# Attention of a two-layer hybrid block: the last ten (head, query block) units of each layer as five two-head units, and the row of maxima in one pass

## The chip, the cores and the metric

The kernel is one program on one core of a Trainium2 chip. The metric is device time in microseconds, from launch to end. All tensors are fp32 in DRAM. TensorE multiplies, VectorE and ScalarE read its results from PSUM, GpSimd does work on SBUF, and SyncE (SP) issues nearly all DMAs.

## The reference

Two layers (`DEPTH = 2`) work on 256 context tokens followed by 2048 latent tokens of width 1024. Each layer is normalised and modulated, projected, and run through three groups of heads in parallel: a bidirectional SSD (6 heads), a bidirectional gated delta rule (4 heads), and attention with 6 query heads of 64 over 2 key/value heads. The mixed result is projected back and added. In the second layer only the latent rows are needed. The attention is plain:

```
def block(qi):
    s = jnp.einsum('bqhgd,bkhd->bhgqk', qi, k).astype(jnp.float32) * scale
    pr = jax.nn.softmax(s, axis=-1).astype(v.dtype)
    return jnp.einsum('bhgqk,bkhd->bqhgd', pr, v)
```

Latent queries see all 2304 keys (18 tiles of 128). Context queries see the 256 context keys, and are computed in layer 0 only.

## The kernel before, in words

The order of a layer is: projections (L389 to L487) in three groups of tokens; gating, preparation and triangular solve of the delta rule (`gdn_pre`, `gdn_solve`); the SSD (`ssd_states`, `ssd_out`); the serial delta-rule chain (`gdn_chain`, 18 steps of two half steps each); the output projection (`load_mix`, `project`, `finish`). Attention is a generator whose units the program emits around the chain: eight units before it, the rest behind it. The order in which each engine gets its instructions is made by the framework's scheduler, which plays the program through with a timeline of its own and gives instructions emitted earlier the higher priority; `tc.high_priority()` raises what stands in it. Each engine then works through its list in that order and waits on semaphores.

A unit of attention is one head with 512 queries against 18 key tiles. There are 24 units of latent queries in each layer (4 query blocks by 6 heads), listed in `big`, and six small ones of context queries in layer 0. A unit has two parts.

`unit_max` (L516) finds the maxima of the scores. For each of 4 query tiles it makes five pieces of scores with the queries as the stationary operand (L531, four of 512 keys and one of 256), reduces each along the keys on VectorE (L533), reduces the five (L535), negates (L536), and turns the four columns of negated maxima into one row by fp32 matmuls against the identity (L541), which VectorE copies into row 64 of `qm` (L542). `qm` holds the first 64 rows of the queries' high and low parts (copied by GpSimd, L522) with that row below; `klo` has a row of ones there. So the second score matmul of `unit_main` subtracts the maximum as it adds the correction for the split of the keys.

`unit_main` (L545) goes over the 18 key tiles: two score matmuls in fp32r (L562, L563) into a PSUM slot, the exponential on ScalarE (L565) into `pe`, and the product with V into `po` (L556), one PSUM bank of its own. V has 65 columns per head; the 65th is ones, so row 64 (or 0) of `po` is the sum of the exponentials. Up to unit 12 that product is one fp32 matmul, which the hardware runs as two instructions. From unit 13 on, `pe` is split into a rounded part `ph` on ScalarE (L570) and a rest `pl` on VectorE (L571), V is split once into `vh[0]` and `vh[1]`, and the product is three fp32r matmuls.

While unit i runs its main part, the maxima of unit i+1 are advanced step by step (`adv`), so that they are spread over its first 14 key tiles. Scores, maxima and the row of maxima share PSUM slots: three banks in `ps_s`, and for the first units a fourth in `ps_x`. After the unit, `po` is copied (L579), and its rows go out by DMA to `mx_d` and `sm_d`; after six units `inv` takes the reciprocals of the sums.

The chain (`gdn_chain`, `load`, `prep`, `step`) loads its data two steps ahead (`kqc`, `acv`, L1034 to L1055), scales `kqc` on VectorE (L1060), and passes a state through TensorE, VectorE and ScalarE in each half step. `behind(mm, prev)` (L1002) fixes the order of two matmuls without a semaphore.

`ssd_states` (L789) has matmuls with 64 output columns, the two groups written to the lower and the upper 64 partitions of one PSUM bank. `identr` is the identity in fp32r, used to transpose in the projections (L326).

## Time and profile before

| | |
|---|---|
| runs | 3998.72, 4003.42, 4008.57 us; median 4003.42 |
| the profiled execution | 3989.31 us, of which the span of instructions is 3987.5 |
| TensorE busy | 3758.9 us, 94% of the span |
| VectorE, ScalarE, GpSimd busy | 2704.5 (68%), 1799.1 (45%), 1347.3 (34%) |
| granted TensorE clock, mean | 0.975 |

PE is TensorE, PEld its weight loads, DVE VectorE, ACT ScalarE, POOL GpSimd, SP SyncE. A matmul's end in the trace is modelled and includes its way through the array, so successive matmuls overlap in the list; the distance between their starts says what one costs in a full queue. "idle before" is the time for which the engine stood still ahead of the instructions of a row, with what released them.

### The profile page before, as it was taken

Reading aid. Unit: us, or ns where it says so; the run is one execution under the profiler, and the core shown is the slowest. Engines: PE = TensorE matmul, PEld = TensorE weight load, DVE = VectorE, ACT = ScalarE, POOL = GpSimd, SP = SyncE. Lnnn points to the kernel's source line nnn. Section 1 sums busy time; section 2 is a strip of 40 time slices with the busy share of each in tenths; the row PEclk is TensorE's granted clock in tenths of the full one; section 3 lists DMA queues with packets and bytes.
Section 4 is the critical chain, followed back from the end, with each engine's and each line's share of the span. In section 5 each row is a group of like instructions: output and inputs, shape, how many; then the busy total and the mean of one; then the engine's idle time right before and its main releaser. Section 6 shows DMA issues by size and latency. Waiting matters only on the chain. (4 is left out here: it accounts for less than half of the span.)

```text
span 3987.5 us, 70354 instructions
## 1 busy us (share of the span) xinstructions
PE 3758.9 (94%) x25750; PEld 2817.7 (71%) x25750; DVE 2704.5 (68%) x5372; ACT 1799.1 (45%) x3728; POOL 1347.3 (34%) x1762
## 2 busy tenths in 40 slices
PE   7999999988999898898999999999989999999989
PEld 5899999554466565565678999996544666656667
DVE  7556474789878566784547574755889876777733
ACT  5343342433466465574214443423333665566710
POOL 5112030376477322412213040302874662133010
PEclk8999999999999999998999999999999999999999
DMA  6343432354222654535744433332442226454244
GB/s 204 99 142 117 135 101 98 96 152 150 72 61 59 121 130 111 134 90 159 240 149 131 149 113 125 119 109 68 148 147 86 59 59 140 110 129 101 82 143 154
DMA packets 549798, 477.72 MB, mean 120 GB/s; under 512 B 133128, under 2 KB 487372, under 8 KB 549452
## 3 DMA queue, kind: packets, MB, share of 16 engines
q1 hardware_dynamic: 507596, 437.82, 37.6%
q10 hardware_dynamic: 41856, 35.40, 2.9%
q8 instruction: 203, 3.33, 0.3%
q14 instruction: 143, 1.17, 0.1%
HBM read 328.91 MB, written 144.18 MB: 119 GB/s over the span
## 5 line engine op out<-in xcount | busy, mean ns | idle before, releaser
L565 ACT ACTIVATE pe<-pst 128x512 f32<-128x512 f32 (+1 forms) x876 | 512.2, 594 | 619.7 <-PE pst L563 588.7
L533 DVE TENSOR_REDUCE mx<-pq 128x1 f32<-128x512 f32 (+1 forms) x972 | 589.5, 626 | 115.7 <-PE pq L531 112.0
L531 PE MATMUL pq<-khh,q 128*128 128x512 f32 (+1 forms) x972 | 456.6, 498 | 43.6 <-DVE mx L533 38.2
L556 PE MATMUL po<-pe,v 128*65 128x512 f32 x960 | 489.0, 598 | 1.8 <-ACT os__11676 L579 1.2
L562 PE MATMUL pst<-q,khh 128*128 128x512 f32 (+1 forms) x876 | 429.0, 490 | 25.5 <-DVE mx L533 23.2
L455 PE MATMUL ps<-lo,wh 128*128 128x384 f32 (+2 forms) x1296 | 441.2, 340 | 0.0
L455 PE MATMUL ps<-hi,wl 128*128 128x384 f32 (+2 forms) x1296 | 441.0, 340 | 0.0
L455 PE MATMUL ps<-hi,wh 128*128 128x384 f32 (+2 forms) x1296 | 440.9, 340 | 0.0
L401 PE MATMUL ps<-wh,hi 128*128 128x320 f32 (+1 forms) x1120 | 354.2, 318 | 1.3 <-DVE hi L365 1.2
L563 PE MATMUL pst<-qm,klo 65*128 65x512 f32 (+1 forms) x876 | 353.8, 405 | 0.0
L401 PE MATMUL ps<-wh,lo 128*128 128x320 f32 (+1 forms) x1120 | 350.0, 315 | 0.7 <-DVE lo L366 0.7
L401 PE MATMUL ps<-wl,hi 128*128 128x320 f32 (+1 forms) x1120 | 350.6, 314 | 0.0
L571 DVE TENSOR_TENSOR pl<-pe,ph 128x512 fp32r<-128x512 f32 x396 | 296.7, 755 | 72.3 <-ACT ph L570 38.2
L531 PEld LDWEIGHTS pq<-khh,q 128*128 128x128 f32 x972 | 184.8, 192 | 205.5 <-DVE mx L533 84.3
L376 DVE TENSOR_TENSOR wl<-wt,wh 128x1024 fp32r<-128x1024 f32 (+3 forms) x144 | 176.4, 1254 | 159.4 <-ACT wh L375 159.4
L570 ACT CAST ph<-pe 128x512 fp32r<-128x512 f32 x396 | 242.9, 620 | 61.0 <-DVE pl L571 21.9
L562 PEld LDWEIGHTS pst<-q,khh 128*128 128x128 f32 x876 | 168.4, 192 | 135.3 <-issue 53.9
L556 PE MATMUL po<-ph,vh 128*65 128x512 f32 x792 | 256.4, 405 | 1.3 <-ACT ph L570 0.7
L455 PEld LDWEIGHTS ps<-lo,wh 128*128 128x128 f32 x1296 | 244.0, 188 | 10.7 <-issue 0.4
L455 PEld LDWEIGHTS ps<-hi,wl 128*128 128x128 f32 x1296 | 243.4, 188 | 10.4
L455 PEld LDWEIGHTS ps<-hi,wh 128*128 128x128 f32 x1296 | 243.5, 188 | 10.3
L1238 PE MATMUL psd<-woh,mh 128*128 128x512 f32 x544 | 220.9, 406 | 18.1 <-ACT mh L1229 16.6
(588 smaller groups left out, 8094.2 us busy)
## 6 DMA issues: line engine op xcount, KB each, us to landing
wt<-in_w_in_dram SPq DMA_DIRECT2D x72, 512.0 KB
wmt<-in_w_mod_dram SPq DMA_DIRECT2D x48, 512.0 KB
pre_d<-pre SPq DMA_DIRECT2D x34, 512.0 KB
acv<-pre_d SPq DMA_DIRECT2D x34, 512.0 KB
kqc<-kt_d SPq DMA_DIRECT2D x68, 256.0 KB
acv<-pre_d SPq DMA_DIRECT2D x68, 256.0 KB
wt<-in_w_in_dram SPq DMA_DIRECT2D x24, 668.0 KB
wt<-in_w_in_dram SPq DMA_DIRECT2D x24, 640.0 KB
```

What stands on the lines that cost most here:

```text
L376: nc.vector.tensor_tensor(out=wl[:, ks, :], in0=wt, in1=wh[:, ks, :].bitcast(F32), op=ALU.subtract)
L401: nc.tensor.matmul(ps, hh[:, k, a], ww[:, k, :], start=(n == 0), stop=(n == 3 * KD - 1))
L455: nc.tensor.matmul(ps, ww[:, k, m * P:(m + 1) * P], hh[:, k, s0:s0 + sn], start=(n == 0), stop=(n == 3 * KD - 1))
L531: nc.tensor.matmul(pq[:, :n], q2[:, u * P:(u + 1) * P], khh[:, kvh, k0t * P + a:k0t * P + a + n], start=True, stop=True)
L533: nc.vector.tensor_reduce(mx[:, i:i + 1], pq[:, :n], axis=AX.X, op=ALU.max)
L556: nc.tensor.matmul(po[0:65, :qn], v[:, kt, vs], p[:, :qn], start=(kt == k0t and j == 0), stop=(kt == k1t - 1 and j == len(ops) - 1))
L562: nc.tensor.matmul(pt[:, :qn], khh[:, kvh, ks], q2[:, :qn], start=True, stop=False)
L563: nc.tensor.matmul(pt[:, :qn], klo[:, kvh, ks], qm[:, :qn], start=False, stop=True)
L565: nc.scalar.activation(out=pe[:, :qn], in_=pt[:, :qn], func=AF.Exp, scale=0.125)
L570: nc.scalar.copy(out=ph, in_=pe)
L571: nc.vector.tensor_tensor(out=pl, in0=pe, in1=ph.bitcast(F32), op=ALU.subtract)
L1238: nc.tensor.matmul(ps, a, w[k][:, n * 512:n * 512 + 512], start=(k == 0 and i == 0), stop=(k == KD - 1 and i == 2))
```

## The change

1. `big[:14]` stay units of one head, all with the whole-fp32 product. `big[14:]` become five pairs of heads (`pair_max`, `pair_main`). The split of `pe` and V, and the pool for it, go.
2. A pair uses one `po` bank: head 0 in partitions 0 to 63, head 1 in 64 to 127, each an fp32 matmul with 64 columns of V. Products are made in visits: once three key tiles are waiting, the two oldest are multiplied, four matmuls one after the other, at high priority and ordered behind the second score matmul of the current tile.
3. V's column of ones is not used by pairs. VectorE adds the two heads' exponentials of each key tile into `acc` (128x1024), and at the end two matmuls with ones sum over the partitions.
4. In `unit_max`, one reduction over all query tiles with `negate` writes the maxima into column 64 of a zeroed fp32r tile (`nmz`), four fp32r matmuls against `identr` turn it into a row, and ScalarE copies the row.
5. `qm` gets its 64 rows by a DMA from `qt_d`; `q2` and `qm` have four buffers instead of three; `pe` has six of 128x1024 instead of four of 128x512.
6. `attention` steps over units of one or two heads; a small unit counts six steps of maxima instead of three.

```diff
@@ -33,6 +33,8 @@
+PB = 6
+NS = 14
 
...
@@ -491,8 +493,6 @@
-            spl = splx.enter_context(tc.tile_pool(reuse_waits="tile", name="spl", bufs=2))
-            vh = []
...
@@ -513,64 +513,59 @@
 
+            nmz = [ap_.tile([P, 4, 65], F32R, name=f"nmz{i}", bufs=1) for i in range(2)]
+            for i in range(2):
+                nc.gpsimd.memset(nmz[i].bitcast(F32), 0.0)
+            turn = iter(range(1000))
+
             def unit_max(h, q0, qn, k0t, k1t, st):
                 kvh = h // 3
-                q2 = ap_.tile([P, 512], F32R, name="q2", bufs=3)
+                q2 = ap_.tile([P, 512], F32R, name="q2", bufs=4)
+                qm = ap_.tile([65, 512], F32R, name="qm", bufs=4)
                 with tc.high_priority():
                     nc.sync.dma_start(q2[:, :qn].bitcast(F32), qt_d[:, h, q0:q0 + qn])
-                qm = ap_.tile([65, 512], F32R, name="qm", bufs=3)
-                nc.gpsimd.tensor_copy(qm[0:64, :qn], q2[0:64, :qn].bitcast(F32))
+                    nc.sync.dma_start(qm[0:64, :qn].bitcast(F32), qt_d[0:64, h, q0:q0 + qn])
                 st.update(q2=q2, qm=qm)
                 kn = (k1t - k0t) * P
                 pieces = [(a, min(512, kn - a)) for a in range(0, kn, 512)]
-                nm = ap_.tile([P, 4], F32, name="nm")
-                for u in range(qn // P):
-                    mx = ap_.tile([P, 8], F32, name="mx", bufs=4)
+                nu = qn // P
+                mx = ap_.tile([P, 4, 5], F32, name="mx", bufs=2)
+                for u in range(nu):
                     for i, (a, n) in enumerate(pieces):
                         pq = aslot("pq")
                         nc.tensor.matmul(pq[:, :n], q2[:, u * P:(u + 1) * P], khh[:, kvh, k0t * P + a:k0t * P + a + n],
                                          start=True, stop=True)
-                        nc.vector.tensor_reduce(mx[:, i:i + 1], pq[:, :n], axis=AX.X, op=ALU.max)
+                        nc.vector.tensor_reduce(mx[:, u, i:i + 1], pq[:, :n], axis=AX.X, op=ALU.max)
                         yield
-                    nc.vector.tensor_reduce(nm[:, u:u + 1], mx[:, 0:len(pieces)], axis=AX.X, op=ALU.max)
-                nc.vector.tensor_scalar(out=nm[:, :qn // P], in0=nm[:, :qn // P], scalar1=-1.0, scalar2=None, op0=ALU.mult)
+                nz = nmz[next(turn) % 2]
+                nc.vector.tensor_reduce(nz[:, 0:nu, 64:65], mx[:, 0:nu, 0:len(pieces)], axis=AX.X, op=ALU.max, negate=True)
                 for _ in range(3):
                     yield
                 pm = aslot("pm")
-                for u in range(qn // P):
-                    nc.tensor.matmul(pm[64:65, u * P:(u + 1) * P], nm[:, u:u + 1], ident, start=True, stop=True)
-                nc.vector.tensor_copy(qm[64:65, :qn], pm[64:65, :qn])
+                for u in range(nu):
+                    nc.tensor.matmul(pm[0:65, u * P:(u + 1) * P], nz[:, u, :], identr, start=True, stop=True)
+                nc.scalar.copy(out=qm[64:65, :qn], in_=pm[64:65, :qn])
                 yield
 
-            def unit_main(h, q0, qn, k0t, k1t, st, sp=()):
+            def unit_main(h, q0, qn, k0t, k1t, st):
                 kvh = h // 3
                 q2, qm = st["q2"], st["qm"]
                 po = ps_o.tile([P, 512], F32, name="po", tag="po")
                 pend = []
 
                 def pv():
-                    kt, pe, ph, pl = pend.pop(0)
-                    vs = slice(kvh * 64, kvh * 64 + 65)
-                    ops = [(v1, pe)] if ph is None else [(vh[0], ph), (vh[1], ph), (vh[0], pl)]
-                    for j, (v, p) in enumerate(ops):
-                        nc.tensor.matmul(po[0:65, :qn], v[:, kt, vs], p[:, :qn], start=(kt == k0t and j == 0),
-                                         stop=(kt == k1t - 1 and j == len(ops) - 1))
+                    kt, pe = pend.pop(0)
+                    nc.tensor.matmul(po[0:65, :qn], v1[:, kt, kvh * 64:kvh * 64 + 65], pe[:, :qn], start=(kt == k0t), stop=(kt == k1t - 1))
 
                 for kt in range(k0t, k1t):
                     ks = slice(kt * P, (kt + 1) * P)
                     pt = aslot("pst")
                     nc.tensor.matmul(pt[:, :qn], khh[:, kvh, ks], q2[:, :qn], start=True, stop=False)
                     nc.tensor.matmul(pt[:, :qn], klo[:, kvh, ks], qm[:, :qn], start=False, stop=True)
-                    pe = ap_.tile([P, 512], F32, name="pe", bufs=4)
+                    pe = ap_.tile([P, 2, 512], F32, name="pe", bufs=PB)[:, 0]
                     nc.scalar.activation(out=pe[:, :qn], in_=pt[:, :qn], func=AF.Exp, scale=0.125)
-                    ph = pl = None
-                    if kt in sp:
-                        ph = spl.tile([P, 512], F32R, name="ph", bufs=2)
-                        pl = spl.tile([P, 512], F32R, name="pl", bufs=2)
-                        nc.scalar.copy(out=ph, in_=pe)
-                        nc.vector.tensor_tensor(out=pl, in0=pe, in1=ph.bitcast(F32), op=ALU.subtract)
-                    pend.append((kt, pe, ph, pl))
-                    if len(pend) > (3 if sp else 1):
+                    pend.append((kt, pe))
+                    if len(pend) > 1:
                         pv()
                     yield
                 while pend:
...
+            def pair_max(h0, q0, qn, k0t, k1t, st):
+                st.update(q2=[], qm=[])
+                gens = []
+                for j in range(2):
+                    sj = {}
+                    g = unit_max(h0 + j, q0, qn, k0t, k1t, sj)
+                    for i, _ in enumerate(g):
+                        if i == 0:
+                            st["q2"].append(sj["q2"])
+                            st["qm"].append(sj["qm"])
+                        yield
+
+            def pair_main(h0, q0, qn, k0t, k1t, st):
+                kvh = (h0 // 3, (h0 + 1) // 3)
+                po = ps_o.tile([P, 512], F32, name="po", tag="po")
+                half = (slice(0, 64), slice(64, 128))
+                pend, acc = [], None
+
+                def visit(n, behind_mm):
+                    with tc.high_priority():
+                        for v in range(n):
+                            kt, pe = pend.pop(0)
+                            for j in range(2):
+                                c0 = kvh[j] * 65
+                                mm = nc.tensor.matmul(po[half[j]], v1[:, kt, c0:c0 + 64], pe[:, j], start=(kt == k0t), stop=(kt == k1t - 1))
+                                if v == 0 and j == 0:
+                                    behind(mm, behind_mm)
+
+                for kt in range(k0t, k1t):
+                    ks = slice(kt * P, (kt + 1) * P)
+                    pe = ap_.tile([P, 2, 512], F32, name="pe", bufs=PB)
+                    for j in range(2):
+                        pt = aslot("pst")
+                        nc.tensor.matmul(pt, khh[:, kvh[j], ks], st["q2"][j], start=True, stop=False)
+                        mm = nc.tensor.matmul(pt, klo[:, kvh[j], ks], st["qm"][j], start=False, stop=True)
+                        nc.scalar.activation(out=pe[:, j], in_=pt, func=AF.Exp, scale=0.125)
+                        if j == 0:
+                            yield
+                    if kt == k0t:
+                        pass
+                    elif kt == k0t + 1:
+                        acc = ap_.tile([P, 2, 512], F32, name="acc", bufs=1)
+                        nc.vector.tensor_tensor(out=acc, in0=pend[0][1], in1=pe, op=ALU.add)
+                    else:
+                        nc.vector.tensor_tensor(out=acc, in0=acc, in1=pe, op=ALU.add)
+                    pend.append((kt, pe))
+                    if len(pend) == 3:
+                        visit(2, mm)
+                    yield
+                visit(len(pend), mm)
+                os_ = ap_.tile([P, 512], F32, name="os2", bufs=1)
+                nc.scalar.copy(out=os_, in_=po)
+                pl = aslot("pl")
+                for j in range(2):
+                    nc.tensor.matmul(pl[half[j]], cc("ones")[:, 0:64], acc[:, j], start=True, stop=True)
+                sm_ = ap_.tile([65, 512], F32, name="sm_", bufs=1)
+                nc.scalar.copy(out=sm_, in_=pl[0:65])
+                for j in range(2):
+                    nc.sync.dma_start(sm_d[None, HQ * q0 + (h0 + j) * qn:HQ * q0 + (h0 + j + 1) * qn], sm_[64 * j:64 * j + 1])
+                nc.sync.dma_start(mx_d[640 + h0 * 64:768 + h0 * 64, q0:q0 + qn], os_)
                 yield
 
...
@@ -623,8 +680,9 @@
-                sb, ss_ = [{} for _ in big], [{} for _ in small]
-                mb = [unit_max(*un, st) for un, st in zip(big, sb)]
+                units = [(1, un) for un in big[:NS]] + [(2, un) for un in big[NS::2]]
+                sb, ss_ = [{} for _ in units], [{} for _ in small]
+                mb = [(unit_max if n == 1 else pair_max)(*un, st) for (n, un), st in zip(units, sb)]
                 ms = [unit_max(*un, st) for un, st in zip(small, ss_)]
 
...
@@ -646,30 +704,28 @@
                 with tc.high_priority():
                     for _ in mb[0]:
                         pass
-                for i, un in enumerate(big):
-                    if i == 13:
-                        for _ in range(2):
-                            vh.append(spl.tile([P, NT, 129], F32R, name=f"vh{len(vh)}", bufs=1))
-                        nc.scalar.copy(out=vh[0], in_=v1)
-                        nc.vector.tensor_tensor(out=vh[1], in0=v1, in1=vh[0].bitcast(F32), op=ALU.subtract)
-                    spn = () if i < 13 else range(NT)
+                at = 0
+                for i, (n, un) in enumerate(units):
                     nxt = ms[i:i + 1] + mb[i + 1:i + 2]
-                    left = (21 + 3) * (i + 1 < len(big)) + 3 * (i < len(small))
+                    left = (24 * units[i + 1][0] if i + 1 < len(units) else 0) + 6 * (i < len(small))
+                    steps = n * (NT - 4)
                     done = 0
-                    for j, _ in enumerate(unit_main(*un, sb[i], spn)):
-                        want = left * (j + 1) // (NT - 4)
+                    for j, _ in enumerate((unit_main if n == 1 else pair_main)(*un, sb[i])):
+                        want = left * (j + 1) // steps
                         adv(nxt, want - done)
                         done = max(done, want)
                     adv(nxt, 99)
                     if i < len(small):
                         for _ in unit_main(*small[i], ss_[i]):
                             pass
-                    if i >= 14:
-                        next(side_work, None)
-                    if i % HQ == HQ - 1:
-                        if small and i == HQ - 1:
+                    at += n
+                    for k in range(at - n, at):
+                        if k >= 14:
+                            next(side_work, None)
+                    if at % HQ == 0:
+                        if small and at == HQ:
                             inv(0, LC)
-                        inv(big[i][1], 512)
+                        inv(un[1], 512)
                     yield
                 for _ in side_work:
                     pass
```

## Rows read from the trace of the kernel before

**Rows 1.** The page: busy us (share of the span) and instructions of each engine.
```profile
PE 3758.9 (94%) x25750; PEld 2817.7 (71%) x25750; DVE 2704.5 (68%) x5372; ACT 1799.1 (45%) x3728; POOL 1347.3 (34%) x1762
```

**Rows 2.** Windows: start:end, length, busy (x instructions) PE PEld DVE ACT POOL, clock, DMA.
```profile
1000.00:1342.00 342.00, 333.52 (x1409) 198.54 (x1408) 272.05 (x578) 184.99 (x487) 206.64 (x240) 0.99 0.23 66
1342.00:1723.00 381.00, 338.70 (x4905) 225.24 (x4904) 265.11 (x499) 225.79 (x442) 116.34 (x103) 0.96 0.56 125
1723.00:1828.00 105.00, 101.91 (x492) 66.96 (x488) 80.30 (x134) 80.09 (x137) 4.55 (x4) 0.98 0.23 73
...
3320.00:3685.00 365.00, 332.53 (x4746) 221.69 (x4746) 259.42 (x484) 220.76 (x433) 105.28 (x95) 0.97 0.53 124
3685.00:3803.00 118.00, 113.97 (x563) 78.02 (x562) 82.31 (x142) 82.97 (x142) 6.44 (x6) 0.99 0.22 72
...
1342.00:1828.00 486.00, 440.61 (x5393) 292.20 (x5392) 345.41 (x632) 305.88 (x579) 120.89 (x107) 0.96 0.49 114
3320.00:3803.00 483.00, 446.50 (x5306) 299.70 (x5304) 341.74 (x625) 303.73 (x574) 111.71 (x100) 0.97 0.46 111
```

**Rows 3.** One line, L579, layer 0: duration min/median/max, first to last start.
```profile
L579 ACT COPY os__17034<-po x1: 583/583/583, 1342.0 to 1342.0; 65x512 f32<-65x512 f32 x1
...
L579 ACT COPY os__20327<-po x1: 582/582/582, 1828.0 to 1828.0; 65x512 f32<-65x512 f32 x1
```

**Rows 4.** Lines, 1342 to 1828: busy us, mean ns | idle before, released by.
```profile
L571 DVE TENSOR_TENSOR pl<-pe,ph 128x512 fp32r<-128x512 f32 x198 | 149.1, 759 | 27.8 <-ACT ph L570 12.6 <-PE po L556 11.6 <-ACT pe L565 1.0
...
L570 ACT CAST ph<-pe 128x512 fp32r<-128x512 f32 x197 | 120.8, 620 | 33.4 <-DVE pl L571 15.6 <-PE po L556 10.5 <-DVE sso L1156 1.0
L533 DVE TENSOR_REDUCE mx<-pq 128x1 f32<-128x512 f32 (+1 forms) x199 | 120.2, 628 | 10.4 <-PE pq L531 9.8
...
L556 PE MATMUL po<-pl,vh 128*65 128x512 f32 x198 | 82.6, 417 | 18.7 <-DVE pl L571 17.8
...
L1060 DVE TENSOR_TENSOR kqc<-kqc,er 128x512 f32<-128x512 f32 x18 | 12.5, 693 | 47.3 <-DMA kqc<-kt_d 44.4 <-DMA er<-eg_d 2.2 <-DMA xt__13036<-xd_d 0.7
...
L610 DVE TENSOR_TENSOR wol<-ws,woh 128x1024 fp32r<-128x1024 f32 x8 | 9.7, 1222 | 2.6 <-ACT woh L609 2.6
```

**Rows 5.** Lines, 3320 to 3803.
```profile
L556 PE MATMUL po<-pl,vh 128*65 128x512 f32 x198 | 81.3, 411 | 13.8 <-DVE pl L571 13.0 <-DMA o_d<-ox 0.4
...
L1060 DVE TENSOR_TENSOR kqc<-kqc,er 128x512 f32<-128x512 f32 x18 | 12.8, 712 | 36.2 <-DMA kqc<-kt_d 32.5 <-DMA er<-eg_d 3.5 <-issue 0.2
```

**Rows 6.** Timeline of PE, a split key tile: start us, us, what.
```profile
1784.79 0.39 PE L562 MATMUL pst<-q,khh 128*128 128x512 f32 x1
1785.03 0.39 PE L563 MATMUL pst<-qm,klo 65*128 65x512 f32 x1
1785.25 0.63 PE L556 MATMUL po<-ph,vh 128*65 128x512 f32 x2
1785.72 0.39 PE L556 MATMUL po<-pl,vh 128*65 128x512 f32 x1
1785.95 0.62 PE L556 MATMUL po<-ph,vh 128*65 128x512 f32 x2
```

**Rows 7.** Timeline of PE, a whole-fp32 product and the row of maxima.
```profile
1033.80 1.02 PE L556 MATMUL po<-pe,v 128*65 128x512 f32 x2
1034.26 0.79 PE L562 MATMUL pst<-q,khh 128*128 128x512 f32 x1
1034.98 1.03 PE L541 MATMUL pm<-cst,nm 128*1 128x128 f32 x8
```

**Rows 8.** Timeline of PE, two short windows: a 256-column maximum, then column halves.
```profile
938.75 0.28 PE L531 MATMUL pq<-khh,q 128*128 128x256 f32 x1
938.97 0.38 PE L789 MATMUL pst<-xd,bn 128*64 128x192 f32 x2
...
939.18 0.33 PE L789 MATMUL pst<-xd,bn 128*64 128x192 f32 x2
```

**Rows 9.** Timeline of PE: three fp32r transposes of 128 columns.
```profile
72.32 0.37 PE L326 MATMUL ptq<-identr,hl 128*128 128x128 f32 x3
```

More of the change, by code (lines that the diff above doesn't have):

```diff
@@ new lines, in pair_main @@
+            def pair_main(h0, q0, qn, k0t, k1t, st):
[32 more added lines that the diff above has]
+                        visit(2, mm)
+                    yield
+                visit(len(pend), mm)
[9 more added lines that the diff above has]
+                nc.sync.dma_start(mx_d[640 + h0 * 64:768 + h0 * 64, q0:q0 + qn], os_)
```

## The prediction, made before the changed kernel was run

> **What bounds the kernel now.** I began with the page: TensorE is busy 94% of the span, VectorE 68%, ScalarE 45% [rows 1]. So an edit is worth what it takes from TensorE, or from what TensorE waits for. Next the windows by stage. The last eleven attention units of a layer (index 13 to 23, which I call the tail) run from 1342 to 1828 us in layer 0 and from 3320 to 3803 us in layer 1: 486 and 483 us, TensorE busy 441 and 447 of them, VectorE 345 and 342, ScalarE 306 and 304; the granted clock is 0.96 and 0.97, so nearly always the upper level of 2.4 GHz [rows 2]. The copies of `po` mark the units: the first of the tail begins as unit 12 is copied at 1342.0, and unit 23 is copied at 1828.0, 44 us per unit [rows 3]. Each tail has two stretches. In the first (381 and 365 us) the delta-rule chain runs between the units; in the second (105 and 118 us) attention stands with the weight split and the first output rows, and TensorE is busy 97% of it [rows 2].
>
> The lines of the tail say what is there: `pl` is 149 us of VectorE, `ph` 121 of ScalarE, the maxima 120 of VectorE; TensorE idled 17.8 and 13.0 us ahead of the products with `pl`, and VectorE idled 47.3 and 36.2 us ahead of the chain's `kqc`, mostly for its DMA [rows 4, 5]. The first stretch thus has three brakes, TensorE's queue, VectorE's queue and those transfers; the second has TensorE.
>
> **The change, part by part.** All durations are of the profiled execution: 3987.5 us of span, 3989.3 in all.
>
> *P times V on TensorE.* Starts of successive matmuls give what one costs in a full queue. A split head's key tile begins at 1784.79 with two score matmuls, its three products run from 1785.25 to 1785.95: 0.23 us per score, 0.70 for P times V [rows 6]. A whole-fp32 product is two instructions: from 1033.80 to 1034.98 run two of them and one score, so 1.18 - 0.23 = 0.95, less some 0.09 for the turn to another kind of matmul = 0.86 us [rows 7]. For two heads in the two column halves, the nearest rows are the chunk states of the SSD, 128x64 in fp32 on either half: two instructions together last 0.38 us, as long as one, and the next two start 0.21 us later [rows 8]. They run side by side. Were 0.21 us for 192 columns to grow with the columns, 512 would take 0.56, and the two passes 1.12 us per key tile of a pair; if only the stream counts, as in the single product, 0.86. I take 0.88, near the single product, since a stream of 512 columns leaves longer to load the next weights. Before, a pair of heads cost 1.40: -0.52 us on 90 key tiles of pairs = -47 us per layer (-25 at 1.12).
>
> The Trainium skill ("TensorE: Matmul & The Clock Gate", section "Why this matters for your kernels") says that three narrow column tiles together reach 2.38 times one, not three times. By that efficiency (0.79) the pair would take 0.86 x 2 / 1.59 = 1.08 us, an estimate from that page, and the saving would be 29 us per layer; the rows of 192 columns fit that, no row here has 512.
>
> *Losses on TensorE.* Unit 13 goes from split (0.70) to plain fp32 (0.86): 18 x 0.16 = +3. The five sums over the partitions are one more fp32 product pair each: 5 x 0.88 = +4. Turning to column halves: the 256-column maximum at 938.75 lets the halves start at 938.97, 0.22 us, where 256 columns stream in about 0.12; some 0.1 into the halves, and I count half as much back, for 45 visits and 5 sums: 50 x 0.15 = +7.5 [rows 8].
>
> *Maxima row.* The eight instructions of `pm` start 0.109 us apart (1.03 us for eight, the last lasting 0.27), 0.87 us per unit [rows 7]. Four fp32r transposes of 128 columns stand in their place; three such took 0.37 us, so some 0.06 each [rows 9], 0.3 us with spread. That is -0.55 us per unit: -5.5 per tail, and -17 us in both layers for the 28 units and six small ones ahead of the tails. There TensorE is busy 333.5 of 342 us [rows 2], so I count the 17 in full. Its reductions and the negation become one instruction, and the row's copy goes to ScalarE, which has room. The copy of `qm` leaves GpSimd for a second DMA of 128 KB on SP, ahead of need like that of `q2`. For pairs the four `q2` buffers are all in use, so the next pair's first load starts only when the pair before is done; it is used within a few tiles, so I count up to 2 us of wait for each of ten pairs, inside the waits below.
>
> *TensorE's sum per tail:* -47 + 3 + 4 + 7.5 - 5.5 = -38 us.
>
> *VectorE.* `pl` goes (149), 85 sums of 128x1024 come; the nearest row is the split of the output weights, 1.22 us [rows 4], 1.25 with traffic = 106. So -43 us, and less small reductions. But look at a pair's first 14 key tiles, into which the next pair's 40 maxima are spread: before, VectorE had 40 x 0.628 + 28 x 0.759 = 46.4 us there and TensorE 28 x 1.16 + 8.4 = 40.9; after, VectorE has 25.1 + 14 x 1.25 = 42.6, TensorE 14 x (0.92 + 0.88) + 8.4 = 33.6. VectorE sets that part: -3.8 per pair. In the last four tiles TensorE does: 9.3 to 7.2. So -5.9 per pair, -29 us per tail, if nothing but attention ran. With the chain between, TensorE has more of its own and the -38 is nearer. I take -35 per tail.
>
> *Waits.* TensorE's 30.8 us ahead of `pl` go. In their place come the exponential of the last key tile, the sum behind it, the load named above, and maxima that sit behind a 1.25 us add; I put these at the same 31 us. ScalarE loses 121 us of `ph` per tail and gets little; it is not what is waited for, so nothing.
>
> *Sum:* -35 x 2 - 17 = -87 us: 3902 in terms of the profiled execution. The median of the runs is 4003.42, 1.0035 of it, so 3916, rounded to 3915.
>
> **Rivals.**
> *Half the gain.* In the first stretch VectorE waits at `kqc` for DMAs while maxima and sums stand behind it, so that stretch keeps its length, and only the second gives: 10 us per layer from TensorE, some 10 for what attention got ahead, and 10 for the maxima rows: -50, 3955. For it: the 47.3 and 36.2 us of idle time [rows 4, 5]. Against: attention is a filler there, and cheaper filler finishes more units before the chain ends. The Trainium skill ("TensorEngine Tiling (Array Packing)", section "Performance Considerations") warns that tiling speeds TensorE up and leaves the PSUM copies as they were; here that is the 42.6 us of VectorE against 33.6 worked out above.
>
> *More.* ScalarE and VectorE answer the chain sooner without `ph` and `pl`, and the tail shrinks with VectorE's load: (345 - 50) / 345 of 485 us is -70 per layer; -157 in all, 3847. For it: both tails were slowed by all three engines. Against: the DMAs do not shrink.
>
> *Slower: the chain is held up.* The visits have priority over the chain and put four fp32 products, 1.76 us, ahead of whatever it has ready, and an add of 1.25 us ahead of its VectorE steps. The chain has 36 half steps per layer, one after another. It ends 105 us before the tail does [rows 2], so it decides from 105 us of delay, 2.9 us a half step. At 3.5 us it ends 21 us late per layer; less the 17: +25, 4028. Against: a split unit already put bursts of 0.70 us and 0.76 us subtractions there, and was itself long.
>
> *The halves run one after another.* Then a pair's key tile takes 1.72, not 1.40: +29 per tail, against -5.5 for `pm` and -15 of waits for `pl`; with the losses and the 17 it comes to about +15, 4018. Against: the equal starts in [rows 8].
>
> **How the numbers follow.** Forecast 0.47, half 0.20, more 0.14, chain held up 0.10, one after another 0.05, no net effect for reasons not named 0.04. The forecast's own range is 3885 to 3940 (the 1.12 end and the -29 above it, waits gone without successors below it). For 8 in 10 I reach from the upper half of "more" past "half the gain": 3840 to 3990. A measurement of this kernel can tell 0.3%, 12 us, from no change. Faster by more: 0.47 + 0.19 + 0.14 = 0.80; slower by more: 0.10 and half of 0.05, 0.12; the rest, 0.08, within.
>
> **What would show it.** In the profile after: starts of the halves' products in pairs, with the next pair some 0.43 us later (0.56 and the saving halves; 0.86 apart and alone means serial); TensorE's idle time ahead of `pl` gone and little in its place; the adds at 1.2 to 1.3 us; the row of `pm` four instructions 0.06 us apart; the tails 35 us shorter each, the stretch before them by about 8 per layer. A chain stretch longer than 381 and 365 us would speak for the slower rival, an unchanged one for the half gain; VectorE's idle time at `kqc` tells them apart from the forecast.

## The result, and the profile after

The changed kernel takes 4026.84 us, median of 6 runs (4016.11 to 4030.72); the kernel before took 4002.67 in 6 runs. The ratio is 1.0057, 95% interval [1.0041, 1.0074]: slower by some 24 us, where 87 us less were forecast. The profiled execution of after took 4030.72 us, span 4028.9, 41 us more than that of before; its mean granted clock is 0.951 of 2.4 GHz, before 0.975.

On the page of after, the busy times (us, share of the span, instructions) and TensorE's granted clock in 40 slices of the span:

```profile
PE 3751.1 (93%) x25190; PEld 2735.7 (68%) x25190; DVE 2579.9 (64%) x4886; ACT 1599.2 (40%) x3384; POOL 1325.6 (33%) x1712
...
PEclk9999999899999988899999999998999999987999
```

VectorE has lost 125 us and ScalarE 200 against [rows 1], and the span grew: the work went, waits came. TensorE's 3751 us look unchanged, but many of its instructions now run at a lower clock and so last longer.

By stage (start:end, length, then busy time of PE, PEld, DVE, ACT, POOL, granted clock, DMA share, GB/s), after: the chain, attention behind it, and the output stage, in layer 0 and layer 1:

```profile
1370.00:1797.00 427.00, 365.22 (x4879) 214.97 (x4880) 256.78 (x402) 159.04 (x328) 112.10 (x96) 0.85 0.55 117
1797.00:1838.00 41.00, 39.72 (x156) 17.70 (x155) 31.60 (x32) 28.74 (x50) 4.99 (x3) 1.00 0.41 135
1838.00:2113.00 275.00, 249.84 (x1051) 183.76 (x1052) 128.07 (x173) 63.00 (x84) 63.34 (x42) 0.95 0.65 205
3379.00:3782.00 403.00, 358.11 (x4756) 207.82 (x4754) 250.01 (x393) 158.42 (x326) 102.58 (x93) 0.88 0.52 119
3782.00:3819.00 37.00, 35.58 (x154) 16.89 (x148) 28.95 (x30) 27.13 (x47) 3.98 (x3) 1.00 0.43 142
3819.00:4029.00 210.00, 187.38 (x778) 145.79 (x772) 73.38 (x116) 19.77 (x34) 16.16 (x16) 0.96 0.48 152
```

The output stages before, with the same columns:

```profile
1828.00:2091.00 263.00, 236.99 (x990) 172.65 (x991) 128.09 (x168) 60.17 (x79) 62.17 (x42) 0.94 0.65 207
3803.00:3987.00 184.00, 163.49 (x664) 129.07 (x663) 67.21 (x108) 15.99 (x28) 16.20 (x16) 0.94 0.49 159
```

What answers to [rows 2] is this. The chain stretch is 427 and 403 us at a clock of 0.85 and 0.88, where its first stretch before was 381 and 365 at 0.96 and 0.97 (from the chain's own first step it took 401 and 387). The rest of attention behind it fell from 105 and 118 us to 41 and 37. And the output stage grew by 12 and 26 us. Attention ends 10 us later in layer 0 (1838, not 1828) and takes 2 us less in layer 1; with the output stages, and projections of layer 1 that are 4 us shorter, this makes the 41 us to within rounding: 10 + 12 - 4 - 2 + 26 = 42.

TensorE's longest waits in the tail of layer 0, 1370 to 1838 us of after (who waited, for whom; us in total, times, longest), and VectorE's:

```profile
PE pq L536 <- DVE mx L538: 24.7, 11, 5.0
PE pst L613 <- DVE mx L538: 19.8, 6, 6.1
PE p L1160 <- DVE Sc L1187: 7.7, 4, 4.9
```

```profile
DVE acv L1121 <- DMA acv<-pre_d: 47.9, 16, 5.1
DVE mx L538 <- PE pq L536: 42.1, 50, 3.7
DVE acc L624 <- ACT pe L615: 28.7, 32, 3.3
DVE kqc L1116 <- DMA kqc<-kt_d: 15.8, 12, 3.1
```

The same views of before, 1342 to 1828 us, TensorE and VectorE:

```profile
PE po L556 <- DVE pl L571: 17.8, 13, 4.5
PE pq L531 <- DVE mx L533: 8.2, 6, 1.9
...
PE pst L562 <- DVE mx L533: 1.3, 1, 1.3
```

```profile
DVE kqc L1060 <- DMA kqc<-kt_d: 44.4, 15, 4.6
DVE acv L1065 <- DMA acv<-pre_d: 13.6, 6, 4.2
```

The wait for `pl` [rows 4] is gone, and TensorE now waits 44.5 us for maxima where it waited 9.5. VectorE stands idle ahead of the chain's two scalings as long as before (78.7 us in all, before 80.8), now most of it at `acv` in place of `kqc`. What such a stop does is seen in the timeline of after near 1602 us (start, duration, engine, what, idle before), VectorE first, then TensorE:

```profile
1604.41 0.69 DVE L1121 TENSOR_TENSOR acv<-acv,msk 128x512 f32<-128x512 f32 x1 [4.07 <-DMA er<-eg_d]
1605.02 0.68 DVE L538 TENSOR_REDUCE mx<-pq 128x1 f32<-128x512 f32 x1
```

```profile
1602.08 0.51 PE L536 MATMUL pq<-khh,q 128*128 128x512 f32 x1
...
1605.76 0.80 PE L536 MATMUL pq<-khh,q 128*128 128x512 f32 x1 [3.18 <-DVE mx L538]
1606.35 0.63 PE L613 MATMUL pst<-q,khh 128*128 128x512 f32 x1
1606.78 0.63 PE L614 MATMUL pst<-qm,klo 65*128 65x512 f32 x1
1607.34 3.68 PE L604 MATMUL po<-pe,v 128*64 128x512 f32 x8
1610.95 0.37 PE L1160 MATMUL p<-Sc,kqc 64*64 64x64 f32 x2
```

VectorE's queue is in order: it stood 4.07 us at the scaling of `acv`, with a maximum behind it. TensorE idled 3.18 us for it (by the program, because attention's three PSUM slots were full), and behind that stop its score matmuls last 0.63 us and start 0.43 apart, at 1.2 GHz (the granted clock from 1606 to 1610 us is 0.50); at 2.4 GHz they last 0.39 and start 0.24 apart [rows 6]. All eight stops of 3 us or more in this tail were followed by the lower level; before has two such stops. In the whole tail the clock stood at 1.2 GHz for 126 us, before for 34.

### The profile page after: what moved, and what is told of

Same layout as the page of the kernel before. It is cut to its first block, busy times and chain, and to the rows that moved or that the text cites. A ratio compares the mean times of both kernels' runs of the same rounds, so it can differ in the third digit from the quotient of the medians.

```text
span 4028.9 us, 68036 instructions
## 1 busy us (share of the span) xinstructions
PE 3751.1 (93%) x25190; PEld 2735.7 (68%) x25190; DVE 2579.9 (64%) x4886; ACT 1599.2 (40%) x3384; POOL 1325.6 (33%) x1712
## 5 line engine op out<-in xcount | busy, mean ns | idle before, releaser
L536 PE MATMUL pq<-khh,q 128*128 128x512 f32 (+1 forms) x972 | 477.2, 531 | 88.3 <-DVE mx L538 78.2
L558 PE MATMUL po<-pe,v 128*65 128x512 f32 (+1 forms) x1032 | 533.4, 605 | 2.4 <-ACT os__11633 L574 1.2
L566 ACT ACTIVATE pe<-pst 128x512 f32<-128x512 f32 (+1 forms) x516 | 300.2, 591 | 465.5 <-PE pst L564 462.0
L615 ACT ACTIVATE pe<-pst 128x512 f32<-128x512 f32 x360 | 206.3, 598 | 281.2 <-PE pst L614 277.8
L563 PE MATMUL pst<-q,khh 128*128 128x512 f32 (+1 forms) x516 | 284.8, 553 | 31.3 <-DVE mx L538 29.3
L624 DVE TENSOR_TENSOR acc<-acc,pe 128x1024 f32<-128x1024 f32 x160 | 207.6, 1298 | 60.3 <-ACT pe L615 58.5
L1294 PE MATMUL psd<-woh,ml 128*128 128x512 f32 x544 | 218.2, 403 | 2.4 <-DVE ml L1287 1.3
L1294 PE MATMUL psd<-wol,mh 128*128 128x512 f32 x544 | 218.1, 401 | 0.0
L377 ACT CAST wh<-wt 128x1024 fp32r<-128x1024 f32 (+3 forms) x144 | 145.8, 1056 | 173.4 <-PE ps L457 150.7
```

The costliest lines, as they stand in the source:

```text
L377: nc.scalar.copy(out=wh[:, ks, :], in_=wt)
L536: nc.tensor.matmul(pq[:, :n], q2[:, u * P:(u + 1) * P], khh[:, kvh, k0t * P + a:k0t * P + a + n], start=True, stop=True)
L558: nc.tensor.matmul(po[0:65, :qn], v1[:, kt, kvh * 64:kvh * 64 + 65], pe[:, :qn], start=(kt == k0t), stop=(kt == k1t - 1))
L563: nc.tensor.matmul(pt[:, :qn], khh[:, kvh, ks], q2[:, :qn], start=True, stop=False)
L566: nc.scalar.activation(out=pe[:, :qn], in_=pt[:, :qn], func=AF.Exp, scale=0.125)
L615: nc.scalar.activation(out=pe[:, j], in_=pt, func=AF.Exp, scale=0.125)
```

## The experiments

Each ratio is to the kernel before on the same chip. That kernel's median lay between 4002.16 and 4006.77 us from chip to chip, so two kernels are compared by their differences to it: `own` is +2 us, `max_row` -24, `scale_on_gpsimd` -105. `own` stands for the changed kernel with the pool edit of the first experiment, on which most of the others build.

**A pool of their own for the new tiles.** Edit: a pool `app` besides `ap`.

```diff
-pe = ap_.tile([P, 2, 512], F32, name="pe", bufs=PB)
+pe = app.tile([P, 2, 512], F32, name="pe", bufs=PB)   # acc, os2, sm_ too
```

> The changed kernel with pe, acc, os2 and sm_ in a pool of their own, so that the pool of q2, qm and mx stays short; nothing else differs. Theory 1 (the longer pool pushes the first unit's query loads and maxima behind the end of the projections, which costs some 20 us in each layer): the first maxima start near 560 us again, the first copy of po comes some 40 us after the projections end instead of 64, and the time falls by about 40 us to 3985, 0.995 of before. Rival (the late start is made up for later, since the same work is only moved): first maxima near 560, the time stays at 4020 to 4030. Both expect the granted clock of the chain stretches to stay near 0.86.

4004.49 us; 1.0007 [0.9997, 1.0017]: 22 us of the loss is where the tiles lie, about half of the 40 expected. When SyncE issues the first two `q` loads of layer 0, before, after and `own`:

```profile
554.04 1.34 SPq L520 DMA_DIRECT2D q<-qt_d  x3
```

```profile
701.51 1.83 SPq L526 DMA_DIRECT2D q<-qt_d  x4
```

```profile
552.81 0.90 SPq L527 DMA_DIRECT2D q<-qt_d  x2
```

With the large tiles in `ap`, the loads stand behind the projections (which end at 703 in after, and so again in layer 1), and the first unit's `po` is copied at 767.4, not 744.4 as in `own` (750.0 before).

**The maxima row alone.** The kernel before with the new `unit_max` and nothing else.

```diff
 # kernel before
-def unit_max(...)   # four reductions, nm, eight passes of pm
+def unit_max(...)   # as in after: nz, four transposes, second DMA
```

> The kernel before with the maxima row in one pass alone: one reduction, four fp32r matmuls, the row copied by ScalarE, qm by DMA, four buffers of q2 and qm. Units and their split stay as before. Forecast of the sum in the prediction: 17 us for the units ahead of the tails and 11 in the tails, so 3975 to 3990, 0.993 to 0.997 of before. Rival (this edit costs time by itself, by ScalarE's copy or the second load): 4003 or more.

3978.57 us; 0.9936 [0.9919, 0.9953]. This part gave 24 us; the prediction's terms for it sum to 28 (17, and 5.5 in each tail). Four transposes of after, start to start 0.06 us (first and last start, x4):

```profile
L546 PE MATMUL pm<-identr,nmz x4: 224/226/274, 3765.3 to 3765.5; 128*65 128x128 f32 x4
```

**The pairs alone.** `own` with the old `unit_max` (four buffers each of `q2` and `qm`).

```diff
 # own
-def unit_max(...)   # as in after
+def unit_max(...)   # as before
```

> The kernel before with the pairs alone (own pool for pe, acc, os2, sm_; four buffers of q2 and qm; all units up to 13 whole fp32), the maxima row as before. If the parts add, as measured so far: max_row took 24 us off, own_pool with both stands where before does, so pairs alone cost about 26 us: 4020 to 4035, clock of the chain stretches 0.86 to 0.88. Rival (the maxima row's new form and the pairs hinder each other): within 10 us of before, or faster.

4064.42 us; 1.0142 [1.012, 1.0163]. Pairs on their own cost 58 us; beside the new maxima row they cost 26 (2 + 24). The parts do not add: with pairs the row edit is worth 55 us, without them 24.

**The chain's two scalings on GpSimd.** The waits for `kqc` and `acv` leave VectorE's queue.

```diff
 # own
-nc.vector.tensor_tensor(out=kq[:, 0], in0=kq[:, 0], in1=er, ...)
+nc.gpsimd.tensor_tensor(out=kq[:, 0], in0=kq[:, 0], in1=er, ...)
-nc.vector.tensor_tensor(out=acv[:, :, 0], ...msk...)
+nc.gpsimd.tensor_tensor(out=acv[:, :, 0], ...msk...)
```

> As own_pool, and the chain's scaling of kqc by er and masking of acv run on GpSimd instead of VectorE, so that VectorE does not stand still for the chain's loads. Theory 2 (VectorE waits 3 to 5 us for those loads with maxima behind it, TensorE runs out of PSUM slots and stands still, and its clock falls to 1.2 GHz): the granted clock of the chain stretches rises from about 0.86 to 0.95 or more, TensorE's waits for mx fall from 44 us to under 20 in layer 0, and the time falls 40 to 80 us below own_pool. Rivals (VectorE's adds or the priority of the visits are the brake): clock and time within 15 us of own_pool.

3897.11 us; 0.9732 [0.9711, 0.9753], 107 us below `own`, more than the 40 to 80 expected. Its chain stretches, and TensorE's longest two waits in 1371 to 1777:

```profile
1371.00:1753.00 382.00, 349.66 (x4908) 205.59 (x4906) 242.37 (x364) 164.73 (x340) 163.47 (x135) 0.92 0.61 130
3313.00:3669.00 356.00, 331.95 (x4767) 197.95 (x4768) 239.20 (x355) 160.12 (x330) 154.03 (x128) 0.95 0.59 134
```

```profile
PE pq L537 <- DVE mx L539: 10.0, 5, 6.1
PE p L1175 <- DVE r L1165: 7.5, 2, 3.8
```

Waits for maxima fall from 38.2 us in `own` (24.6 and 13.6) to 10.0, the clock rises from 0.86 and 0.89 to 0.92 and 0.95, and the chain takes 382 and 356 us, not 426 and 405. The edit also takes 28 us of work per tail off VectorE (18 times 0.820 and 0.734 us), but that cannot be what it is worth: 104 us of adds per tail, left out below, gave 25 us.

**The same edit on the three other kernels.** On after, on the kernel before, and on the maxima row alone:

```diff
 # after / before / max_row: the two lines nc.vector -> nc.gpsimd
-nc.vector.tensor_tensor(...)
+nc.gpsimd.tensor_tensor(...)
```

> The changed kernel itself with one edit: the scaling of kqc and the masking of acv on GpSimd. scale_on_gpsimd (3897) has the pool of its own besides. If VectorE's waits for the chain's loads cost the changed kernel what they cost own_pool (107 us) and the late first unit stays worth 22 us: 3912 to 3930, the clock of the chain stretches 0.91 to 0.95. If the two hang together (the late start brings the stalls): over 3960.

> The kernel before with the scaling of kqc and the masking of acv on GpSimd, as in scale_on_gpsimd, nothing else. It tells whether that edit helps any kernel or the pairs above all. Theory 2 (a split unit rides over VectorE's waits, a pair does not): clock of the chain stretches 0.97 as before, 10 to 40 us faster, 3962 to 3992. Rival (VectorE's waits cost both kernels alike): about 105 us faster, 3897.

> max_row with the scaling on GpSimd: the same as scale_on_gpsimd but for the pairs, which are split single units here. The difference to scale_on_gpsimd (3897) is what the pairs are worth where VectorE does not wait for loads. Theory 2 and the prediction's sum (29 to 38 us per layer): 3950 to 3970. Rival (the pairs give nothing in any case): 3890 to 3905.

3924.2 us, 0.9803 [0.9785, 0.982]; 3929.9, 0.9825 [0.981, 0.9841]; 3913.14, 0.9778 [0.9764, 0.9791]. Their differences to before are -81, -74 and -91 us. So the edit is worth 105 and 107 us where attention runs in pairs (after, `own`), 74 and 68 where it is split (before, `max_row`): the wait cost both kernels, the pairs 31 to 40 us more. For before that lies between the two expectations; for `max_row` it is nearer to the rival, by which the pairs give nothing. With it gone, pairs are worth 14 us (-105 against -91): their sign turns, but their size stays far below the 70 of the sum.

**The sums left out.** `own` without the adds to `acc` (a constant is divided by, so the weights are not normalised), and the same beside the GpSimd edit.

```diff
-nc.vector.tensor_tensor(out=acc, in0=pend[0][1], in1=pe, op=ALU.add)
-else:
-    nc.vector.tensor_tensor(out=acc, in0=acc, in1=pe, op=ALU.add)
+nc.gpsimd.memset(acc, 1.0)
```

> As own_pool, but the 17 adds of each pair on VectorE are left out (acc is filled with ones by GpSimd, so the sums of the exponentials of the last ten heads are not computed). Theory 2: VectorE still waits for the chain's loads, the clock of the chain stretches stays below 0.92, and the time is at most 20 us below own_pool. Rival 3 (the 1.3 us adds on VectorE are the brake): TensorE's waits for mx nearly go, clock 0.95 or more, 50 us or more below own_pool.

> scale_on_gpsimd without the adds on VectorE (sums of the last ten heads not computed). What VectorE's adds cost where it does not wait for loads. If VectorE's load is the second brake on the pairs: 25 us or more below scale_on_gpsimd (3897), chain stretches shorter. If the chain's end and its lag to the output projection set the time: within 12 us of 3897.

3979.1 us, 0.9949 [0.9929, 0.9969], and 3881.42, 0.9685 [0.9668, 0.9702]: 25 and 20 us for 208 us of adds (104.1 of them in one tail, below). That is between what was expected and the rivals; the adds cost something, but are not the main brake.

**The visits' priority.** `visit` without its high priority, in `own` and beside the GpSimd edit.

```diff
-with tc.high_priority():
+with ExitStack():
```

> As own_pool, the visits without high priority, in their order behind the scores as before. Rival 4 (visits ahead of the chain hold it up): chain stretches 20 us or more shorter each, 30 us or more below own_pool (4004), so under 3975. Theory 2: within 15 us of own_pool, the clock of the chain stretches still near 0.86.

> scale_on_gpsimd with the visits at the priority of the other attention work. no_priority was 6 us below own_pool, so 3885 to 3897, chain stretches up to 10 us shorter. If the visits hold the chain up now that nothing else does: 20 us or more below 3897.

3998.83 us, 0.9990 [0.9978, 1.0001], and 3895.09, 0.9723 [0.9702, 0.9745]: 8 and 7 us. The burst of products ahead of the chain is not what makes it longer.

**A fourth PSUM slot for attention.** At the chain, one bank goes from the chain to attention.

```diff
 # own
-banks(0, 4)
+banks(1, 3)
```

> As own_pool, and beside the chain attention has a fourth PSUM slot (one bank in ps_x, every fourth tile goes there) and the chain three instead of four. Theory 2 (TensorE stands still because its three slots hold maxima that VectorE has not read): fewer waits for mx, 38 to some 30 us in layer 0, clock up by 0.01 to 0.04, 5 to 30 us below own_pool, unless the chain suffers from its lost slot. Rivals 3 and 4: no change, or slower.

4053.52 us; 1.0123 [1.0107, 1.0138]. The most telling miss: attention ended 70 us sooner (last `po` of layer 0 copied at 1754, in `own` 1824), the chain, with one bank less, ended 51 us later, and the kernel took 47 us more than `own`. The chain's last state update and the first matmul of the output (source views: durations min/median/max, first to last start) for before, after, this kernel, `pairs_alone` and `scale_on_gpsimd`:

```profile
L1131 DVE TENSOR_TENSOR Sc<-sd,p x36: 406/415/423, 1366.2 to 1730.6; 128x256 f32<-128x256 f32 x36
...
L1238 PE MATMUL psd<-woh,mh x236: 388/393/793, 1764.9 to 2054.4; 128*128 128x512 f32 x118
```

```profile
L1187 DVE TENSOR_TENSOR Sc<-sd,p x36: 405/415/422, 1406.9 to 1796.9; 128x256 f32<-128x256 f32 x36
...
L1294 PE MATMUL psd<-woh,mh x225: 387/393/794, 1849.0 to 2069.6; 128*128 128x512 f32 x113
```

```profile
L1188 DVE TENSOR_TENSOR Sc<-sd,p x36: 404/415/422, 1411.8 to 1843.7; 128x256 f32<-128x256 f32 x36
...
L1295 PE MATMUL psd<-woh,mh x227: 387/393/797, 1867.8 to 2069.5; 128*128 128x512 f32 x114
```

```profile
L1183 DVE TENSOR_TENSOR Sc<-sd,p x36: 361/414/422, 1433.4 to 1842.6; 128x256 f32<-128x256 f32 x36
...
L1290 PE MATMUL psd<-woh,mh x206: 387/393/792, 1883.0 to 2069.5; 128*128 128x512 f32 x103
```

```profile
L1188 DVE TENSOR_TENSOR Sc<-sd,p x36: 408/414/422, 1402.7 to 1752.9; 128x256 f32<-128x256 f32 x36
...
L1295 PE MATMUL psd<-woh,mh x288: 387/393/796, 1788.2 to 2050.7; 128*128 128x512 f32 x144
```

In all five the output begins 24 to 52 us behind the chain's end: the weights' pool opens where the chain's closes, their loads are issued 12 to 21 us later, and then they are split. Before, 97 us of attention stood behind the chain's end, covered that gap, and overlapped the first output rows. In the fourth slot nothing covers it: from attention's end at 1754 to the output at 1868 TensorE is busy 52 of 114 us.

The chain's end is not the only thing that holds the output, though. In after the weights were split by 1831, but the load of the first output rows stands in SyncE's queue behind attention's last rows; the output begins at 1849, 11 us behind attention's last copy (1838.1), and TensorE idles 9.9 us ahead of it. And in `max_row` the chain ends 50 us later than before (last update at 1780.7, not 1730.6), while the kernel is 24 us faster.

**All units as plain fp32, no pairs** (`NS = 24`, with the GpSimd edit).

```diff
-NS = 14
+NS = 24
```

> scale_on_gpsimd with no pairs at all: 24 single units, all with the whole-fp32 product (NS = 24). By TensorE's sum a unit costs 18 x 0.86 for P times V, against 18 x 0.70 split and 18 x 0.43 in a pair: 7.7 us more per head than in a pair, 77 us per layer. If TensorE's work set the time: 150 us above scale_on_gpsimd, 4045. If the chain's end sets it: 20 to 70 us above, 3917 to 3967, with the difference in the part behind the chain's end.

3934.11 us; 0.9819 [0.9802, 0.9836]. Without pairs the ten heads take 10 x 18 x 0.43 = 77 us more of TensorE per layer, 155 in all, less 9 for the sums over partitions; VectorE's adds go. The kernel lost 32: of the saving on TensorE that these figures give the pairs (155 - 9), a fifth comes back.

**More pairs** (`NS = 10` and `8`, with the GpSimd edit): pairs also where the SSD runs, ahead of the chain.

```diff
-NS = 14
+NS = 10   # and 8
```

> scale_on_gpsimd with ten single units and seven pairs (NS = 10). Two more pairs take 4 x 18 x 0.43 = 31 us per layer from TensorE, in the stretch ahead of the chain. If the chain's end sets the time, an earlier start of the chain counts in full: the chain starts and ends 15 to 30 us earlier per layer, 3835 to 3875. If VectorE is full there (40 maxima and 17 adds per pair): 3885 to 3905.

> scale_on_gpsimd with eight single units and eight pairs (NS = 8), three more pairs than there. By the chain's end: 3820 to 3865, chain starts 25 to 45 us earlier per layer. By VectorE's load: 3885 to 3920.

3989.76 us, 0.9964 [0.9952, 0.9977], and 4022.35, 1.0038 [1.0025, 1.0051]: 89 and 122 us slower than with 14, where a gain was expected, or a loss of at most 8 and 23 us. The stretch ahead of the chain, 1085 to 1370 us, for `NS` 14, 10 and 8:

```profile
1085.00:1370.00 285.00, 273.80 (x1165) 168.75 (x1162) 225.82 (x461) 165.79 (x445) 172.09 (x187) 0.99 0.20 57
```

```profile
1085.00:1370.00 285.00, 254.56 (x1002) 148.03 (x1001) 241.12 (x442) 142.16 (x384) 155.63 (x154) 0.87 0.17 48
```

```profile
1085.00:1370.00 285.00, 255.03 (x967) 148.45 (x963) 237.32 (x424) 140.35 (x381) 153.87 (x148) 0.83 0.15 46
```

VectorE goes from 226 to 241 and 237 us of 285, TensorE's waits for maxima from 6 to 15 and 16 us, TensorE does fewer instructions at a lower clock, and the chain starts 48 and 60 us later. That points at VectorE's load as the limit here; no run shows it apart from the clock. The Trainium skill ("TensorEngine Tiling (Array Packing)", section "Performance Considerations") says that tiling raises TensorE's pace and not that of the copies out of PSUM; this trace agrees, with the maxima, which read PSUM, in the copies' place (the sums read SBUF).

## Why the prediction was wrong, point by point

- *P times V on TensorE: right.* Forecast 0.88 us per key tile of a pair. In `scale_on_gpsimd`, at full clock, a pair of passes (one in each half) starts 0.43 us behind the pair ahead of it, and a tile has two such pairs, 0.86 us (each row joins the four passes that overlap):

```profile
1506.75 1.03 PE L605 MATMUL po<-pe,v 128*64 128x512 f32 x4
...
1507.18 1.03 PE L605 MATMUL po<-pe,v 128*64 128x512 f32 x4
```

  That is what a single whole-fp32 product takes [rows 7]: two halves of 512 columns run fully side by side. The 1.08 us estimated from the Trainium skill ("TensorE: Matmul & The Clock Gate", section "Why this matters for your kernels") is not borne out here, and the rival of halves one after another is refuted. In after the passes of two tiles fill 1607.34 to 1610.95, 1.8 us a tile, at the lower clock.
- *Maxima row: right* (24 measured, 28 forecast), when it is made alone.
- *VectorE's sums: right in size.* 1301 ns against 1.25 us forecast; 80 of them and the products, after, 1370 to 1838 us:

```profile
L604 PE MATMUL po<-pe,v 128*64 128x512 f32 x360 | 104.3, 673 | 0.0
...
L624 DVE TENSOR_TENSOR acc<-acc,pe 128x1024 f32<-128x1024 f32 x80 | 104.1, 1301 | 29.6 <-ACT pe L615 28.7
```

- *Waits: the step that failed.* "I put these at the same 31 us." That was for both tails; the three waits shown above came to 52 us in layer 0's and to 33 in layer 1's. And that is only what they cost while they last: the sum held no term for the clock behind a stop. Over the whole profiled execution TensorE is idle 278 us, before 229; of its busy time 319 us lie at 1.2 GHz, before 162. If busy time at that level does half the work (an estimate from these figures), the lower clock took 160 us, before 81. So the span's 41 us are 49 more of idle time, 79 more for the clock, and 87 less of work. The work came off about as the prediction's TensorE terms had it (2 x 38 + 17 = 93); idle time and clock took more than all of it. The cause named under *half the gain* (VectorE stands at the chain's loads, with maxima behind) was there, in both kernels and about equally long; I gave it too small a price, perhaps since with cheaper products TensorE has less else to do while VectorE stands. That last step is argued from the two waits tables, not shown by a run of its own. What is shown by moving the two scalings is that VectorE's stops there cost the kernels with pairs 105 to 107 us, and the others 74 and 68.
- *The loads "ahead of need": failed.* They stood behind the projections, in both layers, because of where the larger tiles lay: 22 us, shown by the pool edit. No term was priced for placement.
- *-35 us per tail: failed even without the waits.* Pairs gave 14 us, both layers together, beside the GpSimd edit. The sum took work saved in the tail for time. Between the profiled executions of `max_row_gpsimd` and `scale_on_gpsimd` TensorE's work falls by 41 us (the same estimate), but its idle time grows by 14 and the loss to the clock by 16. That attention ends sooner is not enough by itself, as the fourth slot shows: behind the chain's end it was cover for the output weights.
- *Rival "the chain is held up": half right.* Its place, sign and size (4028, measured 4027) were right, its mechanism was not: the visits' priority costs 8 us and the sums 25; VectorE's stops and placement made most of the loss. That its number came out is luck. The sum of the other slower rival, halves one after another, is wrong in the prediction: with all its terms counted it gives 2 x (29 + 3 + 4 + 7.5 - 5.5 - 15) - 17 = +29, not +15.

The ledger: maxima row -24, placement +22, pairs +26, together +24. It adds up because the parts are taken in this order; with the old maxima row the pairs cost 58. Without VectorE's waits at the loads the pairs are worth -14 beside the new row, so those waits make 40 of the loss.

Open: idle time and lower clock are told apart above by an estimate from the traces, not by a run. Nor is it settled why the chain does not run faster with lighter attention beside it, nor why the parts interact as strongly as they do in `pairs_alone`.

## What to carry to other kernels

Before counting a saving on the busiest engine as time, ask whether that engine will then stand idle and at what clock it will go on: here its work fell about as forecast, and idle time and the lower clock took more than all of it. Ask too whether the work that is saved only covered a gap of the next stage. Look in each in-order queue for an instruction that waits for a DMA with the busy engine's consumers behind it, and move that one first: here two lines moved to GpSimd were worth 68 to 107 us, more than the rewritten attention, and with them the pairs make the fastest version, 3895 to 3897 us, 2.7% below the kernel before. Price the placement of every tile that grows.

## What the hardware showed that I had not expected

- Two heads side by side in column halves, 512 queries in fp32, cost no more than one head's single product of 65 columns: a pair of passes takes 0.43 us and a key tile has two, so 0.86 us for two heads, as for one [rows 7].
- Stops of 3 us in an otherwise full TensorE queue were followed by matmuls at 1.2 GHz (score starts 0.43 us apart, not 0.24). Over the chain stretch of layer 0 the granted clock is 0.85, with 44.5 us of waits for maxima; `scale_on_gpsimd`, with 10.0, has 0.92.
- GpSimd does the two scalings in 1523 and 1300 ns, VectorE in after in 820 and 734, and the kernel gained 107 us by it: the slower engine was the better place, since no maximum for which TensorE waits stands in its queue.
